# Another model of the two DMA queues in an offline planner that orders the instructions of a transformer trunk

## The chip, the core and the metric

The kernel runs on one core of one Trainium2 chip. The core has TensorE (PE, with its weight loads as PEld), VectorE (DVE), ScalarE (ACT), GpSimd (POOL) and SyncE (SP), each of which works through its own list of instructions in order, and 16 DMA engines that move data. Transfers are issued from two queues here: plain loads by SP, and loads that add to what stands in on-chip memory by POOL. The metric is the device time of one execution in microseconds (us).

## The reference, cut to what matters

```python
D_MODEL, SEQ, DEPTH, D_FF, MEM_TOKENS = 1024, 512, 2, 2816, 256
def swiglu(x, w_gate, w_up, w_down):
    return (jax.nn.silu(x @ w_gate) * (x @ w_up)) @ w_down
for i in range(DEPTH):
    x = layer_norm(ALPHA * x + 0.5 * swiglu(x, ffn_w_gate[i, 0], ffn_w_up[i, 0], ffn_w_down[i, 0]), ...)
    x = layer_norm(ALPHA * x + (mixer_ab if i % 2 == 0 else mixer_c)(x, ...), ...)
    x = layer_norm(ALPHA * x + memory_attn(x, mem, ...), ...)
    x = layer_norm(ALPHA * x + 0.5 * swiglu(x, ffn_w_gate[i, 1], ffn_w_up[i, 1], ffn_w_down[i, 1]), ...)
```

All arrays are float32. Layer 0 mixes tokens by global and windowed attention (`mixer_ab`), layer 1 by neighbourhood attention (`mixer_c`). There are thus eight stages: feed-forward, mixer, memory attention, feed-forward, and the same again.

## The kernel before

Every float32 operand is split into a high part `hi` (a CAST on ACT) and a low part `lo` (a subtraction on DVE), and a product is three matmuls: hi·hi, hi·lo, lo·hi.

A feed-forward stage takes the hidden features in pairs of 256 columns. One pair is called a group. The projections of a group (gate, then up) and the group's share of the down projection are each a 2 by 2 block product done with seven block products, in the order 1, 6, 5, 2, 7, 4, 3 (for down 1, 6, 2, 5, 3, 7, 4). Products of the gate or up half alternate on PE with products of the down share of the group before. Four things recur below, by their names in the instructions (the trace leaves the buffer numbers out):

- `a_…` is the PSUM bank of a gate or up product (three banks in rotation), `d_…` and `t_…` are those of down products, `slab_…` is a tile of 128x1024 in on-chip memory, out of 27 in rotation.
- Product 7 of a half ends in a bank; DVE subtracts it (`t<-a,t`, in `quarters`, `mix(own["c22"], ps, own["c22"], ALU.subtract)`), and product 4 may write that same bank only after this subtraction. This is called the handover here.
- A down share (`down_steps`) loads four quarters of its weights by SP, named 11, 12, 22 and 21. Product 2 uses quarter 21: ACT makes its `hi`, DVE its `lo`.
- Two quarters of the gate weights get their `lo` by a POOL transfer that adds the weights in memory to minus `hi` (`wide_late`, `plus`). They are called adds.

The order is not written by hand. `Graph.record` notes every instruction with its dependencies; `Graph.plan` then plays them through with estimated durations, engine by engine, picks at each step the ready instruction with the smallest key, and hands a tile's buffer on to the next tile in line when its last user has ended. `emit` runs `plan` twice: first with the order of recording as the key, then with the latest start that `deadlines` works out. The instructions are issued in the order that results, and so are the buffers given out. All instructions are issued from one line, so the profile shows L157 for nearly everything.

The part of `plan` that concerns a transfer gives each of the two queues (`kind` is true for SP) a start after its issue, a work time by size, and half of its overlap with the other queue on top; its landing is known as soon as it is issued.

Of the kernel before, what the change touches and what calls it, by code (L numbers as in the profile page):

```python
# [47 lines left out]
class Space:  # L48


    def __init__(self, bufs):
        self.bufs = bufs
        self.queue = []


class Recorder:
# [4 lines left out]

    def __getattr__(self, method):
        return lambda *args, **kw: self.graph.record(self.name, method, args, kw)


class Graph:
# [115 lines left out]
    def plan(self):  # L182

        for info in self.tiles.values():
            info["left"], info["at"], info["behind"] = len(info["users"]), 0.0, None
        now = {e: 0.0 for e in self.ENGINES}
        heaps = {e: [] for e in self.ENGINES}
        ready = {e: [] for e in self.ENGINES}
        free = {s: [(0.0, i, None) for i in range(s.bufs)] for s in self.spaces.values()}
        turn = {s: 0 for s in free}  # L190
        queues = {True: [(0.0, 0.0)], False: [(0.0, 0.0)]}
        held, order, table = [0.0, 0.0], [], None
        for op in self.ops:
            op.wait, op.ready = len(op.deps) + len(op.frees), 0.0

        def release(op, t):
            op.ready = max(op.ready, t)
            op.wait -= 1
            if op.wait == 0:
                heapq.heappush(heaps[op.engine], (op.ready, op.key, op.index, op))  # L200

        def grant(space):

            while turn[space] < len(space.queue) and free[space]:
                info = space.queue[turn[space]]
                turn[space] += 1
                if info["users"]:
                    t, _, info["behind"] = heapq.heappop(free[space])
                    for op in info["users"]:
                        release(op, t)  # L210

        def arrive(e):
            while heaps[e] and heaps[e][0][0] <= now[e]:
                _, key, i, op = heapq.heappop(heaps[e])
                heapq.heappush(ready[e], (key, i, op))

        for op in self.ops:
            if op.wait == 0:
                heapq.heappush(heaps[op.engine], (0.0, op.key, op.index, op))
        for space in free:  # L220
            grant(space)
        while len(order) < len(self.ops):
            best = None
            for e in self.ENGINES:
                arrive(e)
                if ready[e] and e in self.PATIENT:
                    key, _, op = ready[e][0]
                    for at, k, _, _ in heapq.nsmallest(4, heaps[e]):
                        if at < now[e] + op.ns * 0.6 and k < key - self.margin:
                            now[e] = at  # L230
                            arrive(e)
                            break
                if ready[e]:
                    t = now[e]
                elif heaps[e]:
                    t = heaps[e][0][0]
                else:
                    continue
                if best is None or t < best[0]:
                    best = (t, e)  # L240
            assert best, "no instruction can start"
            t, e = best
            if not ready[e]:
                now[e] = t
                continue
            _, _, op = heapq.heappop(ready[e])
            shared = lambda pairs, a, b: sum(max(0.0, min(b, y) - max(a, x)) for x, y in pairs)
            stop = t + op.ns
            if op.port:
                stop += max(0.0, held[e == "vector"] - t)  # L250
                held[e != "vector"] = stop
            if op.table and op.table != table:
                stop += 1290.0
                table = op.table
            lands = stop + self.LATENCY[e]
            if op.dma:
                kind = e == "sync"
                work = 250.0 + op.size / 2**19 * 1700.0 if kind else op.size / 2**19 * (4000.0 if op.adds else 1650.0)
                work *= 1.7 if op.thin else 1.0
                begin = max(t + 1040.0 if kind else stop + 2000.0, queues[kind][-1][1])  # L260
                finish = begin + work + 0.5 * shared(queues[not kind][-6:], begin, begin + work)
                queues[kind].append((begin, finish))
                lands = finish + 790.0
            op.start, op.stop, op.lands, now[e] = t, stop, lands, stop
            order.append(op)
            for u in op.users:
                release(u, stop if e == u.engine == "tensor" else lands)
            for info in op.frees:
                info["left"] -= 1
                info["at"] = max(info["at"], lands)  # L270
                if info["left"] == 0:
                    heapq.heappush(free[info["space"]], (info["at"], len(order), info))
                    grant(info["space"])
        return order

    def deadlines(self, order):
# [1417 lines left out]
```

## Time and profile before

| | |
|---|---|
| time, median of 3 runs (lowest, highest) | 2149.89 us (2148.38, 2151.03) |
| time of the profiled execution | 2146.66 us |
| its span in the profile | 2144.9 us |
| PE busy | 2107.5 us, 98% |
| DVE busy | 1688.0 us, 79% |
| ACT busy | 1268.3 us, 59% |
| POOL busy | 403.6 us, 19% |
| DMA moved | 328.43 MB, mean 153 GB/s |

The profile shows one execution. Spans and waits in it are measured from its first instruction, and the execution's own time is 1.8 us more than its span. A PE that is busy 98% of the time leaves 37.4 us in which it does nothing, the start and the end of the kernel included.

### The profile page before, as it was taken

Reading aid. Unit: us, or ns where it says so; the run is one execution under the profiler, and the core shown is the slowest. Engines: PE = TensorE matmul, PEld = TensorE weight load, DVE = VectorE, ACT = ScalarE, POOL = GpSimd, SP = SyncE. Lnnn points to the kernel's source line nnn. Section 1 sums busy time; section 2 is a strip of 40 time slices with the busy share of each in tenths; the row PEclk is TensorE's granted clock in tenths of the full one; section 3 lists DMA queues with packets and bytes.
Section 4 is the critical chain, followed back from the end, with each engine's and each line's share of the span. In section 5 each row is a group of like instructions: output and inputs, shape, how many; then the busy total and the mean of one; then the engine's idle time right before and its main releaser. Section 6 shows DMA issues by size and latency. Waiting matters only on the chain.

```text
span 2144.9 us, 33922 instructions
## 1 busy us (share of the span) xinstructions
PE 2107.5 (98%) x13056; PEld 1888.2 (88%) x13056; DVE 1688.0 (79%) x2480; ACT 1268.3 (59%) x2019; POOL 403.6 (19%) x473
## 2 busy tenths in 40 slices
PE   9999999999999999999999999999999999999997
PEld 7989988888888999889899989888888888999986
DVE  7778888888747888878889878866568477888787
ACT  5655553699546856455765555447765458655552
POOL 1112105410102211111411111312210013111113
PEclk9999999999999999999999999999999999999999
DMA  7787673003443978785887768346554339678762
GB/s 211 178 200 153 172 189 118 20 11 104 143 138 108 206 156 209 177 197 148 202 166 180 165 158 220 94 128 167 129 162 157 130 107 182 157 183 196 175 167 62
DMA packets 261473, 328.43 MB, mean 153 GB/s; under 512 B 12096, under 2 KB 204224, under 8 KB 261312
## 3 DMA queue, kind: packets, MB, share of 16 engines
q1 hardware_dynamic: 178880, 224.28, 33.0%
q0 software_dynamic: 82144, 101.73, 28.4%
q8 instruction: 103, 1.69, 0.3%
q14 instruction: 58, 0.48, 0.1%
q10 hardware_dynamic: 288, 0.26, 0.0%
HBM read 311.55 MB, written 4.19 MB: 147 GB/s over the span
## 4 chain that ended last, share of the span: by engine, by line
PE 81%; DMA 6%; DVE 5%; ACT 4%; issue 2%; POOL 1%; SPq 0%; DVEq 0%; ACTq 0%; POOLq 0%
PE a L157 49%; PE d L157 19%; PE t L157 13%; DMA slab<-ffn_w_down 5%; DVE slab L157 4%; ACT slab L157 2%; ACT t L157 1%; DVE x L157 1%; DVE t L157 1%; DMA slab<-ffn_w_up 1%; POOL slab L157 1%; ACT raw L157 0%; DMA slab<-t 0%; DMA slab<-ffn_w_gate 0%; ACT xh L157 0%
## 5 line engine op out<-in xcount | busy, mean ns | idle before, releaser
L157 DVE TENSOR_TENSOR slab<-slab,slab 128x1024 fp32r<-128x1024 f32 (+3 forms) x586 | 666.7, 1161 | 125.8 <-ACT slab L157 87.5
L157 ACT CAST slab<-slab 128x1024 fp32r<-128x1024 f32 (+2 forms) x516 | 493.8, 984 | 348.2 <-DVE slab L157 124.8
L157 PE MATMUL a<-slab,slab 128*128 128x256 f32 (+2 forms) x2512 | 624.3, 321 | 0.8 <-DMA slab<-t 0.6
L157 PE MATMUL a<-xh,slab 128*128 128x256 f32 (+2 forms) x2384 | 517.9, 307 | 0.5 <-ACT slab L157 0.5
L157 PE MATMUL a<-raw,slab 128*128 128x256 f32 x2432 | 466.9, 286 | 19.6 <-DVE t L157 18.8
L157 PEld LDWEIGHTS a<-slab,slab 128*128 128x128 f32 x2512 | 449.1, 191 | 38.5 <-ACT t L157 1.3
L157 PE MATMUL d<-slab,slab 128*128 128x512 f32 (+2 forms) x1856 | 450.5, 382 | 0.1
L157 PEld LDWEIGHTS a<-xh,slab 128*128 128x128 f32 x2384 | 395.4, 191 | 26.1 <-ACT slab L157 1.1
L157 PEld LDWEIGHTS a<-raw,slab 128*128 128x128 f32 x2432 | 393.3, 194 | 28.4 <-DVE t L157 22.8
L157 PEld LDWEIGHTS d<-slab,slab 128*128 128x128 f32 x1856 | 329.8, 189 | 57.0 <-DVE slab L157 1.3
L157 PE MATMUL a<-xl,slab 128*128 128x256 f32 (+2 forms) x1192 | 366.6, 308 | 0.0
L157 PEld LDWEIGHTS a<-xl,slab 128*128 128x128 f32 x1192 | 227.4, 191 | 14.3 <-DVE xl L157 0.2
L157 PE MATMUL t<-slab,slab 128*128 128x512 f32 (+1 forms) x840 | 209.1, 389 | 1.0 <-DVE x L157 1.0
L157 DVE TENSOR_TENSOR slab<-raw,slab 128x1024 fp32r<-128x1024 f32 (+2 forms) x148 | 160.7, 1105 | 20.0 <-ACT slab L157 19.9
L157 PEld LDWEIGHTS t<-slab,slab 128*128 128x128 f32 x840 | 150.4, 189 | 27.8 <-issue 1.3
L157 POOL DMA_DIRECT2D slab<-ffn_w_gate x63 | 83.3, 1327 | 411.6 <-DVE slab L157 343.9
L157 DVE TENSOR_TENSOR slab<-t,slab 128x512 fp32r<-128x512 f32 (+2 forms) x223 | 137.6, 638 | 17.1 <-ACT slab L157 16.2
L157 POOL DMA_DIRECT2D slab<-ffn_w_up x63 | 81.2, 1337 | 361.3 <-PE a L157 141.5
L157 ACT CAST slab<-t 128x512 fp32r<-128x512 f32 (+2 forms) x223 | 120.5, 564 | 39.7 <-DVE t L157 14.4
L157 ACT CAST slab<-raw 128x1024 fp32r<-128x1024 f32 (+1 forms) x132 | 124.3, 971 | 30.2 <-PE a L157 8.8
L157 DVE SCALAR_TENSOR_TENSOR x<-d,x 128x512 f32<-128x512 f32 x168 | 114.7, 686 | 20.8 <-PE d L157 20.1
L157 ACT COPY t<-a 128x512 f32<-128x512 f32 (+1 forms) x128 | 69.9, 551 | 75.6 <-PE a L157 46.7
(126 smaller groups left out, 2267.8 us busy)
## 6 DMA issues: line engine op xcount, KB each, us to landing
slab<-ffn_w_gate SPq DMA_DIRECT2D x89, 512.0 KB
slab<-ffn_w_up SPq DMA_DIRECT2D x89, 512.0 KB
slab<-ffn_w_down SPq DMA_DIRECT2D x80, 512.0 KB
slab<-ffn_w_gate POOLq DMA_DIRECT2D x63, 512.0 KB, 8.0
slab<-ffn_w_up POOLq DMA_DIRECT2D x63, 512.0 KB, 7.4
slab<-ffn_w_down POOLq DMA_DIRECT2D x40, 512.0 KB, 8.2
raw<-mem_w_kv SPq DMA_DIRECT2D x16, 1024.0 KB
slab<-t SPq DMA_DIRECT2D x96, 128.0 KB
```

Source lines behind the costliest of these rows:

```text
L157: op.call = lambda: fn(*args, **kw)
```

## The change

The planner's estimate of transfers is replaced; nothing else is edited. A class `Flows` keeps each queue as a line of transfers of which the first is served. Alone, it is served at rate 1; with both queues at work, SP's goes at 0.42 and POOL's at 0.6 of it. A 512 KB load has a work of 1530 (SP), 1515 (POOL) or 2900 (POOL, adding), in the planner's nanoseconds; it can begin 1100 after SP's issue begins or 740 after POOL's ends, costs 710 or 800 more when its queue had stood idle, and lands 700 after its work. A transfer's end is now an event of its own: what waits for it is released when the play reaches that time, and not at its issue.

```diff
+class Flows:
+    READY, WORK, RAMP = (1100.0, 740.0), (1530.0, 1515.0, 2900.0), (710.0, 800.0)
+    SHARE = (0.42, 0.6)
...
+    def begin(self, op, pool):
+        at = op.stop + self.READY[1] if pool else op.start + self.READY[0]
+        work = self.WORK[2 if op.adds else int(pool)] * op.size / 2**19
+        self.queues[pool].append([at, work * (1.7 if op.thin else 1.0), op, False])
...
@@ Graph.plan
-        queues = {True: [(0.0, 0.0)], False: [(0.0, 0.0)]}
+        flows = Flows()
...
+            due = flows.due()
+            if due is not None and (best is None or due <= best[0]):
+                op = flows.finish()
+                op.lands = due + 700.0
+                settle(op)
+                continue
...
-            if op.dma:
-                kind = e == "sync"
-                work = 250.0 + op.size / 2**19 * 1700.0 if kind else op.size / 2**19 * (4000.0 if op.adds else 1650.0)
-                work *= 1.7 if op.thin else 1.0
-                begin = max(t + 1040.0 if kind else stop + 2000.0, queues[kind][-1][1])
-                finish = begin + work + 0.5 * shared(queues[not kind][-6:], begin, begin + work)
-                queues[kind].append((begin, finish))
-                lands = finish + 790.0
             op.start, op.stop, op.lands, now[e] = t, stop, lands, stop
             order.append(op)
...
+            if op.dma:
+                flows.begin(op, e == "gpsimd")
+            else:
+                settle(op)
```

`settle` holds what stood here before: it releases the users of an instruction and hands buffers on.

The set of instructions stays. Their order on DVE and ACT changes at many places, on PE at some forty, on POOL at twelve and on SP at seven. Since buffers are handed on in the order of the play, tiles also get other buffers, so a load can wait for another instruction than before. Three places in the second feed-forward stage, in a gate half whose PE part runs from 878 to 905 us in the trace, show the pattern.

On SP, two quarters of down weights (`slab_1775` is quarter 22, `slab_1792` quarter 21) and the up weights behind them, with the semaphores that each waits for, before:

```order
188 L157 DMA slab_1775<-ffn_w_down 128x2x512 [waits DVE_49]
189 L157 DMA slab_1792<-ffn_w_down 128x2x512 [waits DMAHW7_49,DVE_49]
190 L157 DMA slab_1798<-ffn_w_up 128x4x256 [waits DMAHW0_49,PE_49]
191 L157 DMA slab_1801<-ffn_w_up 128x4x256 [waits DMAHW1_49,DMASW7_49,PE_49]
192 L157 DMA slab_1802<-ffn_w_up 128x4x256 [waits DMAHW2_49,DMASW0_49,DVE_49]
```

and after:

```order
188 L218 DMA slab_1775<-ffn_w_down 128x2x512 [waits DMAHW6_49,DVE_49]
189 L218 DMA slab_1792<-ffn_w_down 128x2x512 [waits DMASW5_49,DMAHW7_49,DMASW2_49,PE_49]
190 L218 DMA slab_1798<-ffn_w_up 128x4x256 [waits DMAHW0_49,PE_49]
191 L218 DMA slab_1801<-ffn_w_up 128x4x256 [waits DMAHW1_49,PE_49]
192 L218 DMA slab_1802<-ffn_w_up 128x4x256 [waits DMASW0_49,DMAHW2_49,PE_49,Activation_49]
```

The order on SP is the same here, but the load of quarter 21 waited for DVE (its count is reached by `slab_1790<-slab_1761,slab_1789`) and now waits for PE (its count is reached by the last matmul of product 1, `a_1764<-xl_84,slab_1758` and its neighbour).

On DVE, around the `lo` of quarter 21 (`slab_1795`) and the handover's subtraction (`t_1696_1777<-a_1769,t_1696_1777`), before:

```order
1040 L157 TENSOR_TENSOR slab_1800<-slab_1750,slab_1799 128x1024
1041 L157 TENSOR_TENSOR slab_1795<-slab_1792,slab_1794 128x1024
1042 L157 SCALAR_TENSOR_TENSOR slab_1586<-t_1791,slab_1586 128x512
1043 L157 TENSOR_TENSOR slab_1804<-slab_1798,slab_1803 128x1024
1044 L157 TENSOR_TENSOR t_1696_1777<-a_1769,t_1696_1777 128x512
1045 L157 TENSOR_TENSOR slab_1811<-slab_1798,slab_1801 128x1024
```

and after:

```order
1038 L218 TENSOR_TENSOR slab_1800<-slab_1750,slab_1799 128x1024
1039 L218 TENSOR_TENSOR t_1740_1821<-t_1703_1784,slab_1745 128x512
1040 L218 TENSOR_TENSOR slab_1795<-slab_1792,slab_1794 128x1024
1041 L218 SCALAR_TENSOR_TENSOR slab_1586<-t_1791,slab_1586 128x512
1042 L218 TENSOR_TENSOR t_1696_1777<-a_1769,t_1696_1777 128x512
1043 L218 TENSOR_TENSOR slab_1804<-slab_1798,slab_1803 128x1024
```

The subtraction moved ahead of the low part of an up quarter (`slab_1804`), and a sum of activations (`t_1740_1821`) moved in ahead of `slab_1795`. Further up, `slab_1790` moved ahead of the sum that needs quarter 22 (`slab_1782<-slab_1781,slab_1775`).

On PE, between product 7 (`a_1769<-raw_1534,slab_1790`) and product 4 (`a_1769<-raw_1534,slab_1778`) of the gate half, before:

```order
4979 L157 MATMUL t_1793<-slab_1786,slab_1787 128x512
4980 L157 MATMUL t_1793<-slab_1785,slab_1787 128x512
4981 L157 MATMUL d_1774<-slab_1794,slab_1796 128x512
4982 L157 MATMUL d_1774<-slab_1795,slab_1796 128x512
4983 L157 MATMUL a_1769<-raw_1534,slab_1778 128x256
```

and after:

```order
4974 L218 MATMUL t_1793<-slab_1786,slab_1787 128x512
4975 L218 MATMUL t_1793<-slab_1785,slab_1787 128x512
4976 L218 MATMUL a_1769<-raw_1534,slab_1778 128x256
4977 L218 MATMUL a_1769<-slab_1536,slab_1778 128x256
4978 L218 MATMUL a_1769<-raw_1534,slab_1779 128x256
```

Two matmuls of down product 2 (`d_1774`) stood between `t_1793` and product 4; they now stand behind product 4 with the other four of that product.

More of the change, by code (lines that the diff above doesn't have):

```diff
@@ L63, in __getattr__, with __init__, advance, due @@
         return lambda *args, **kw: self.graph.record(self.name, method, args, kw)
+class Flows:
+    READY, WORK, RAMP = (1100.0, 740.0), (1530.0, 1515.0, 2900.0), (710.0, 800.0)
+    SHARE = (0.42, 0.6)
+    def __init__(self):
+        self.queues, self.idle, self.clock, self.next = ([], []), [0.0, 0.0], 0.0, None
+    def begin(self, op, pool):
+        at = op.stop + self.READY[1] if pool else op.start + self.READY[0]
+        work = self.WORK[2 if op.adds else int(pool)] * op.size / 2**19
+        self.queues[pool].append([at, work * (1.7 if op.thin else 1.0), op, False])
+        self.next = None
+    def advance(self, until):
+        while True:
+            busy, limit = [], until
+            for k, q in enumerate(self.queues):
+                if q and q[0][0] <= self.clock:
+                    if not q[0][3]:
+                        q[0][3] = True
+                        q[0][1] += self.RAMP[k] if self.idle[k] < q[0][0] else 0.0
+                    busy.append(k)
+                elif q:
+                    limit = min(limit, q[0][0])
+            rate = {k: self.SHARE[k] if len(busy) == 2 else 1.0 for k in busy}
+            ends = [(self.clock + self.queues[k][0][1] / rate[k], k) for k in busy]
+            stop = min([limit] + [z for z, _ in ends])
+            for k in busy:
+                self.queues[k][0][1] -= (stop - self.clock) * rate[k]
+            self.clock = stop
+            for z, k in ends:
+                if z <= stop:
+                    return k
+            if stop >= until:
+                return None
+    def due(self):
+        if not self.queues[0] and not self.queues[1]:
+            return None
+        if self.next is None:
+            kept = self.clock, list(self.idle), [[list(z) for z in q[:1]] for q in self.queues]
+            k = self.advance(1e12)
+            self.next = self.clock, k
+            self.clock, self.idle = kept[0], kept[1]
+            for q, z in zip(self.queues, kept[2]):
+                q[:1] = z
+        return self.next[0]
+    def finish(self):
+        self.due()
+        k = self.next[1]
+        self.advance(self.next[0])
+        self.idle[k], self.next = self.clock, None
+        return self.queues[k].pop(0)[2]
 class Graph:
@@ L221, in plan, with settle @@
             grant(space)
-        while len(order) < len(self.ops):
+        def settle(op):
+            for u in op.users:
+                release(u, op.stop if op.engine == u.engine == "tensor" else op.lands)
+            for info in op.frees:
+                info["left"] -= 1
+                info["at"] = max(info["at"], op.lands)
+                if info["left"] == 0:
+                    heapq.heappush(free[info["space"]], (info["at"], len(order), info))
+                    grant(info["space"])
+        while len(order) < len(self.ops) or flows.due() is not None:
             best = None
@@ L246, in plan @@
             _, _, op = heapq.heappop(ready[e])
-            shared = lambda pairs, a, b: sum(max(0.0, min(b, y) - max(a, x)) for x, y in pairs)
             stop = t + op.ns
@@ L255, in plan @@
             lands = stop + self.LATENCY[e]
-            if op.dma:
-                kind = e == "sync"
-                work = 250.0 + op.size / 2**19 * 1700.0 if kind else op.size / 2**19 * (4000.0 if op.adds else 1650.0)
-                work *= 1.7 if op.thin else 1.0
-                begin = max(t + 1040.0 if kind else stop + 2000.0, queues[kind][-1][1])
-                finish = begin + work + 0.5 * shared(queues[not kind][-6:], begin, begin + work)
-                queues[kind].append((begin, finish))
-                lands = finish + 790.0
             op.start, op.stop, op.lands, now[e] = t, stop, lands, stop
             order.append(op)
[L266 to L273, printed above, removed]
+            if op.dma:
+                flows.begin(op, e == "gpsimd")
+            else:
+                settle(op)
         return order
```

## The prediction

> **What bounds the kernel now.** I read the page first, then who PE waits for, then the chain that ended last, then one wait instruction by instruction.
>
> ```profile
> span 2144.9 us, 33922 instructions
> PE 2107.5 (98%) x13056; PEld 1888.2 (88%) x13056; DVE 1688.0 (79%) x2480; ACT 1268.3 (59%) x2019; POOL 403.6 (19%) x473
> ```
>
> PE is the bound, and a change of order can't shorten its work. It can only take from the 37.4 us in which PE is idle. Who ends that idle time (us in total, times, longest):
>
> ```profile
> PE a L157 <- DVE t L157: 18.8, 11, 3.1
> PE a L157 <- ACT t L157: 0.7, 1, 0.7
> PE a L157 <- DMA slab<-t: 0.6, 2, 0.4
> ```
>
> Half of it is one row: eleven waits of a gate or up product for DVE's `t<-a,t`, the handover. The same question for the stretch 1080 to 1200 us gives the two smallest of them:
>
> ```profile
> PE a L157 <- DVE t L157: 1.7, 2, 0.9
> ```
>
> so nine make 17.1, 1.9 each. The chain says why DVE is late (start, length, what), in the gate half of the second feed-forward stage that the change was shown in:
>
> ```profile
> 876.36 1.23 DVE slab L157
> 877.61 6.31 DMA slab<-ffn_w_down
> ...
> 887.50 1.83 DVE slab L157 x2
> 889.35 6.92 DMA slab<-ffn_w_down
> ...
> 896.34 1.06 ACT slab L157
> ...
> 897.42 1.24 DVE slab L157
> ...
> 900.30 0.70 DVE t L157
> ...
> 901.03 1.01 PE a L157 x6
> ```
>
> A load of quarter 21 starts the moment DVE ends its second instruction (887.50 + 1.83), takes 6.92 us, and ACT, DVE and PE follow it. On ACT and DVE it looks like this (idle time before, and its cause, in brackets):
>
> ```profile
> 889.96 1.05 ACT L157 CAST slab<-slab 128x1024 fp32r<-128x1024 f32 x1 [0.33 <-DVE t L157]
> 896.34 1.05 ACT L157 CAST slab<-slab 128x1024 fp32r<-128x1024 f32 x1 [5.34 <-DMA slab<-ffn_w_down]
> ```
> ```profile
> 892.24 1.22 DVE L157 TENSOR_TENSOR slab<-slab,slab 128x1024 fp32r<-128x1024 f32 x1
> 897.42 1.23 DVE L157 TENSOR_TENSOR slab<-slab,slab 128x1024 fp32r<-128x1024 f32 x1 [3.96 <-ACT slab L157]
> 898.56 0.68 DVE L157 SCALAR_TENSOR_TENSOR slab<-t,slab 128x512 f32<-128x512 f32 x1
> 899.16 1.22 DVE L157 TENSOR_TENSOR slab<-slab,slab 128x1024 fp32r<-128x1024 f32 x1
> 900.30 0.69 DVE L157 TENSOR_TENSOR t<-a,t 128x512 f32<-128x512 f32 x1
> ```
> ```profile
> 896.72 0.28 PE L157 MATMUL a<-raw,slab 128*128 128x256 f32 x1
> 896.84 1.55 PE L157 MATMUL t<-slab,slab 128*128 128x512 f32 x6
> 898.23 0.98 PE L157 MATMUL d<-slab,slab 128*128 128x512 f32 x2
> 901.03 0.39 PE L157 MATMUL a<-raw,slab 128*128 128x256 f32 x1 [1.83 <-DVE t L157]
> ```
>
> Product 7 has ended at 897.0, so the subtraction could run then. It stands in DVE's list behind an instruction that waits for ACT, which waits for the load, and starts at 900.30. Nothing in the subtraction needs the load: a list in order blocks it. The chain has the same load at other places of the kind:
>
> ```profile
> 119.43 7.61 DMA slab<-ffn_w_down
> ...
> 952.51 7.20 DMA slab<-ffn_w_down
> ...
> 1968.09 6.80 DMA slab<-ffn_w_down
> ```
>
> By the old formula a 512 KB load lands 1.04 + 1.95 + 0.79 = 3.8 us after its issue when alone; here it takes 6.7 to 7.6. The old play thus had ACT and DVE go on where they stand still.
>
> **The load of quarter 21.** Its new release is the last matmul of product 1:
>
> ```profile
> 881.06 0.28 PE L157 MATMUL a<-xh,slab 128*128 128x256 f32 x1
> ```
>
> That ends at 881.3; the load before it on SP is out at 877.61, so quarter 21 goes out about 8.0 us before 889.35. At its own 6.92 us it lands at 888.3. Among busier neighbours it may take longer; the longest transfer on the chain is this one:
>
> ```profile
> 1090.28 11.90 DMA slab<-ffn_w_up
> ```
>
> At 11.90 it lands at 893.2, still 3.0 before 896.3. ACT is free at 891.0, so its cast ends by 894.3 at worst. The program has the same exchange, PE for DVE, at each of the nine; at 1182 (one of the small two) the release is 4.5 us earlier.
>
> **The order on DVE.** `slab_1804` (1.14 from start to start) leaves the place before the subtraction, `t_1740_1821` (0.60) comes in. Before that, DVE no longer stands still at quarter 22:
>
> ```profile
> 884.01 1.23 DVE L157 TENSOR_TENSOR slab<-slab,slab 128x1024 f32<-128x1024 f32 x1 [1.57 <-DMA slab<-ffn_w_down]
> ```
>
> Played through with these rows: `t_1703`, `t_1751`, `slab_1787` and `slab_1790` now fill this hole and end near 886.0, the sum with quarter 22 ends at 887.1 (before 885.2), the `lo` of product 6 (`slab_1786`) at 889.5 (before 887.6), `slab_1800` at 891.9, `slab_1795` near 893.7 or, with the slowest load, 895.6, the next accumulation by 896.3. DVE is then idle before 897.0, and the subtraction runs from 897.1 to 897.8.
>
> **The order on PE.** The two `d<-slab,slab` (0.45 from start to start) go behind product 4, so PE is at product 4 at 898.23. The margin is 0.4 us. That such a handover costs nothing is seen in an up half, with six matmuls between and the subtraction on time:
>
> ```profile
> 221.91 1.55 PE L157 MATMUL d<-slab,slab 128*128 128x512 f32 x6
> 223.30 0.28 PE L157 MATMUL a<-raw,slab 128*128 128x256 f32 x1
> ```
> ```profile
> 222.11 0.69 DVE L157 TENSOR_TENSOR t<-a,t 128x512 f32<-128x512 f32 x1 [1.05 <-PE a L157]
> ```
>
> Value of each of the nine: its whole wait. From below it is nothing (the load stays where it was), from above its 1.9; I take the upper end, since even the longest transfer lands in time. The two small ones go for the same reasons (at the one DVE's subtraction moved ahead of two low parts, at the other the load is earlier), and so does the 0.7 behind ACT, at 1103: the copy that PE waits for moved ahead of the cast that waits for the 11.90 us transfer.
>
> **The adds.** They now share their time with one more load. The `lo` of product 2 comes by an add issued here, and by the row of its own stretch lands 8.9 us later, at 887.0:
>
> ```profile
> 878.12 1.28 POOL L157 DMA_DIRECT2D slab<-ffn_w_gate  x1 [1.40 <-ACT slab L157]
> ```
> ```profile
> slab<-ffn_w_gate POOLq DMA_DIRECT2D x1, 512.0 KB, 8.9
> ```
> ```profile
> 889.94 0.40 PE L157 MATMUL a<-xh,slab 128*128 128x256 f32 x2
> ```
>
> PE first reads it at 889.94, so it may be 2.9 us later at no cost. Quarter 22 lands at 883.9 (877.61 + 6.31); until then the add shares as before, and of its last 3.1 us a load beside it can take at most as much again if both get half: 890.1. I take no cost and keep 0.2 for each.
>
> [...] An add alone took 5.9 us (139 us), those in company 8.9, so the trace agrees with the sharing; the planner's own 0.6 and 0.42 are near to half.
>
> **New waits.** PE's order also changes at five places without this pattern: the first gate halves near 765 and 1845, a half near 815, two pairs of heads near 1497 and 1542 whose scores now come earlier among other matmuls. PE does not wait at the first three now, and at the heads the row with 0.6 above is all. Nothing from below; from above, five of the longest of the two waits near 1103 and 1109, 0.9, or 4.5. I take 0.4 each, between nothing and 0.9 and near the two single waits that make the 0.6: 2.0. Start and end keep their instructions, with exchanged neighbours (gate and up banks at the start; `x_4` and `x_5` at the end): nothing. Some loads go out later instead of earlier, most a quarter 12 near 802 (and its like near 1145 and 1882), 5.8 us by the instruction that it now waits for. Here are its issue (the second of two) and the sum that reads it:
>
> ```profile
> 801.89 0.97 SPq L157 DMA_DIRECT2D slab<-ffn_w_down  x2
> ```
> ```profile
> 820.48 1.22 DVE L157 TENSOR_TENSOR slab<-slab,slab 128x1024 f32<-128x1024 f32 x1
> ```
>
> The 18 us between them cover 5.8 and a transfer of 11.90: nothing.
>
> **Sum.** -18.8 - 0.7 + 2.0 = -17.5. Against the profiled execution, 2146.66 - 17.5 = 2129.2. The median of the runs lies 3.23 above the profiled execution, so 2132.4.
>
> **Rivals.**
> 1. The adds are slowed more than by half, and PE waits 1 us at product 2 in ten places: -7.5, so 2142.4. For it: add and loads fill the queues in just these stretches. Against: 2.9 us of room.
> 2. The exchange brings nothing, because the load is served late all the same: DVE's order alone gives 1.14 - 0.60 = 0.54, of which the two matmuls that PE no longer has in front take 0.45. Nine times 0.1: 2149.0, no change. It needs a load of over 15 us (881.3 to 896.3), beyond any row above.
> 3. Slower: `slab_1786` is the place. The down product 6 that needs it starts at 892.58, in a row of its own:
>
> ```profile
> 892.58 0.63 PE L157 MATMUL t<-slab,slab 128*128 128x512 f32 x2
> ```
>
> I have it ready at 889.5. If DVE is held by quarter 22 for 3.1 us more, PE waits; each further us costs ten. The gain is gone at 894.3, and at 895.6 the kernel takes 2146.66 + 3.23 - 17.5 + 30 = 2162. For it: two more instructions stand before it now. Against: quarter 22's release is unchanged.
> 4. The five new places cost 2 us each instead of 0.4: 2140.4.
>
> **How the numbers follow.** My case 0.72 (2127 to 2138: the sum with new waits from nothing to 4.5, the 0.2 of the adds, and some 3 either way for the median's offset); rival 1 0.10; rival 2 0.05; rival 3 0.04; rival 4 0.06; better than 2127, 0.03. A measurement here tells about 0.2%, 4.3 us. The range 2127 to 2143 holds my case, rival 4 and most of rival 1. Faster: 0.72 + 0.10 + 0.06 + 0.03, less 0.01 for the far end of rival 1: 0.90. Same: 0.05 of rival 2 and that 0.01. Slower: rival 3, 0.04.
>
> **What would show it.** Right: PE's wait for `t<-a,t` falls from 18.8 to under 3, ACT's and DVE's brackets of 5.34 and 3.96 are gone or under 1, quarter 21 goes out near 881 within its half, PE's idle time falls to about 20. Wrong: a row of PE waiting for an add or for a DVE `slab` of several us, or the old row still above 9.

## The result, and the profile after

The changed kernel takes 2130.8 us (median of 4 runs, 2130.46 to 2132.42); the kernel before, beside it, 2150.15 (4 runs, 2148.38 to 2151.03). The ratio is 0.9913, its 95% interval 0.9895 to 0.9930. The profiled execution takes 2130.46 us, 16.2 less than that of before.

The head of the page after, and the rows of who PE waits for that answer to those shown (us in total, times, longest):

```profile
span 2128.7 us, 33875 instructions
PE 2101.7 (99%) x13056; PEld 1884.8 (89%) x13056; DVE 1692.7 (80%) x2480; ACT 1270.3 (60%) x2019; POOL 405.7 (19%) x473
```
```profile
PE a L218 <- ACT slab L218: 5.7, 1, 5.7
...
PE d L218 <- DMA slab<-ffn_w_up: 2.5, 2, 1.4
PE a L218 <- DVE t L218: 1.5, 2, 1.0
```

PE's idle time fell from 37.4 to 27.0 us, and its busy time by 5.8: together the 16.2. The row of handovers fell from 18.8 (11 times) to 1.5 (2 times), and neither of these two is one of the old eleven. Two other rows are new: one wait of 5.7 us, and 2.5 us for adds (before, PE waited 0.7 at these two places).

The place that was shown, on SP, ACT, DVE and PE (everything is about 6.2 us earlier by now: product 7's last matmul starts at 890.55, before at 896.72):

```profile
871.44 4.01 SPq L218 DMA_DIRECT2D slab<-ffn_w_down  x2
```
```profile
883.52 2.01 ACT L218 CAST slab<-slab 128x1024 fp32r<-128x1024 f32 x2
```
```profile
886.35 1.22 DVE L218 TENSOR_TENSOR slab<-slab,slab 128x1024 fp32r<-128x1024 f32 x1
888.00 0.69 DVE L218 SCALAR_TENSOR_TENSOR slab<-t,slab 128x512 f32<-128x512 f32 x1 [0.43 <-PE t L218]
890.88 0.69 DVE L218 TENSOR_TENSOR t<-a,t 128x512 f32<-128x512 f32 x1 [2.18 <-PE a L218]
```
```profile
890.55 0.28 PE L218 MATMUL a<-raw,slab 128*128 128x256 f32 x1
890.67 1.55 PE L218 MATMUL t<-slab,slab 128*128 128x512 f32 x6
892.06 0.28 PE L218 MATMUL a<-raw,slab 128*128 128x256 f32 x1
```

The second load of the SP row is quarter 21; its issue ends at 875.45. The second of the two casts on ACT is its own and has no bracket: the load has landed. DVE's first row is its low part, done 3.0 us before product 7's last matmul starts. Now DVE waits for PE (2.18) and not PE for DVE: product 4 follows at 892.06 without a bracket.

The chain of waits shows where the 5.7 us come from, in the third feed-forward stage:

```profile
1067.52 1.29 POOL slab L218
1068.81 0.04 issue
1068.85 0.01 POOLq L218
1068.87 14.16 DMA slab<-ffn_w_gate
1083.03 0.02 issue
1083.05 1.05 ACT slab L218
```

Two adding loads stand behind each other in POOL's queue, and the second one, which PE needs first, takes 14.16 us from issue to landing. The planner's play has it land 8.0 us after its issue: of the 166 adding loads of feed-forward weights, the one that comes latest against the play.

A stretch in which PE is granted half its clock follows that wait. One of the four in the kernel before stands behind the wait at 899 us (columns: stretch, us, PE busy, granted clock, DMA share, GB/s). Before, then after:

```profile
901.84:905.25 3.41, 3.41 (x18) 0.50 0.02 5
```
```profile
1083.71:1090.54 6.83, 6.39 (x29) 0.50 0.30 46
```

In the kernel before, the other three begin at 256.7, 1246.6 and 2041.9, each 2.4 to 3.3 us after the start of a handover wait; the changed kernel has this one only. If half of such a stretch is lost at the granted 0.50, that is 6.8 us before and 3.4 after, an estimate, so 3.4 of the 5.8 us that PE's busy time fell by. The other 2.4 I haven't traced.

### The profile page after: what moved, and what is told of

It is laid out like the page before. It is cut to its first block, busy times and chain, and to the rows that moved or that the text cites. A ratio compares the mean times of both kernels' runs of the same rounds, so it can differ in the third digit from the quotient of the medians.

```text
span 2128.7 us, 33875 instructions
## 1 busy us (share of the span) xinstructions
PE 2101.7 (99%) x13056; PEld 1884.8 (89%) x13056; DVE 1692.7 (80%) x2480; ACT 1270.3 (60%) x2019; POOL 405.7 (19%) x473
## 4 chain that ended last, share of the span: by engine, by line
PE 89%; DMA 4%; DVE 2%; issue 2%; ACT 2%; POOL 1%; SPq 0%; DVEq 0%; POOLq 0%; ACTq 0%
PE a L218 54%; PE d L218 20%; PE t L218 14%; DMA slab<-ffn_w_gate 2%; DVE slab L218 1%; DMA slab<-ffn_w_up 1%; ACT slab L218 1%; DVE x L218 1%; POOL slab L218 1%; DMA slab<-ffn_w_down 0%; SPq L218 0%; ACT t L218 0%; DMA raw<-mem_w_kv 0%; POOL x L218 0%; DMA raw<-x_t 0%
## 5 line engine op out<-in xcount | busy, mean ns | idle before, releaser
L218 PE MATMUL a<-raw,slab 128*128 128x256 f32 x2432 | 462.0, 284 | 1.0 <-DVE t L218 1.0
L218 ACT CAST slab<-t 128x512 fp32r<-128x512 f32 (+2 forms) x223 | 120.5, 565 | 48.6 <-PE t L218 18.8
```

The lines of the kernel that those rows point to most:

```text
L218: op.call = lambda: fn(*args, **kw)
```

## Experiments

The theory on record: the load of quarter 21 left too late, so its release makes the nine waits. The rival: the subtraction stands in the wrong place in DVE's list, and the load's time matters little. Eleven kernels, each timed in turns with the kernel before. `again` in the diffs writes the program out once more, each engine in a given order, buffers handed on as they come free (in late_load as the plan gave them).

| kernel | median us | ratio to before, 95% | PE's wait for DVE `t`: us, times |
|---|---|---|---|
| changed kernel | 2130.8 | 0.9913 (0.9895 to 0.9930) | 1.5, 2 |
| late_load | 2134.65 | 0.9923 (0.9895 to 0.9952) | 1.4, 1 |
| later_load | 2130.16 | 0.9904 (0.9880 to 0.9927) | none |
| latest_load | 2173.53 | 1.0106 (1.0083 to 1.0129) | 26.0, 9 |
| early_load | 2142.85 | 0.9968 (0.9955 to 0.9982) | 16.0, 10 |
| sub_mid | 2136.74 | 0.9939 (0.9922 to 0.9956) | 13.2, 10 |
| both | 2122.03 | 0.9874 (0.9856 to 0.9893) | 0.9, 1 |
| early_sub | 2124.62 | 0.9885 (0.9860 to 0.9911) | 5.1, 4 |
| ahead | 2118.97 | 0.9860 (0.9843 to 0.9877) | none |
| swap_adds | 2127.93 | 0.9892 (0.9872 to 0.9913) | 0.7, 1 |
| land_later | 2132.58 | 0.9923 (0.9906 to 0.9940) | 2.2, 2 |
| no_sharing | 2196.44 | 1.0218 (1.0197 to 1.0239) | 35.8, 15 |

**Is it the time of the load? Three doses on the changed kernel.** The load of quarter 21 waits at nine places for a DVE instruction as well; every engine keeps its order. First the instruction that it waited for in the kernel before (late_load):

```diff
-        for op in order:
-            op.call()
...
+        extra = [(loads[a], lows[b]) for a, b in [(278, 276), (369, 367), (460, 458), (1792, 1790), (1883, 1881), ...]]
+        after = dict(extra)
+        order = self.again(order, extra)
+        made = {}
+        for op in order:
+            made[op] = op.call()
+            if op in after:
+                self.tc.add_manual_dep(made[op].ins, made[after[op]].ins.name, ...)
```

> The changed kernel with every engine's order kept, but at the nine places the load of quarter 21 waits again for the DVE instruction that it waited for before (the low part of product 7's weights), so the buffer exchange alone is undone. By the rows of the changed kernel that instruction ends at 879.9 at the place shown, where the load now goes out near 875: 5 us later. At 6.92 us it lands at 886.8, its cast ends by 887.9, its low part by 889.1, the accumulation by 889.8, and the subtraction can't run before product 7 ends at 890.9. So if the slack is what I think, nothing returns: 2131 us (2129 to 2135), PE's wait for DVE t under 3 us. Rival (the exchanged buffer is the whole of the gain, as the prediction put it): the nine waits return, 17 us, 2148.

Measured 2134.65, at the upper end of the range; by the intervals it isn't told apart from the changed kernel. At eight places nothing returns. At the ninth, at 248 us, the load leaves only 7.5 us before product 7's last matmul, and PE waits 1.4. So the exchanged buffer by itself is not the gain. Next a later instruction, `[(278, 272), (369, 363), ...]`, in later_load:

> The same, but the load of quarter 21 waits for the low part of product 6's weights, which ends at 883.4 at the place shown: 7.5 us before the subtraction can run, as the load before went out 7.65 us before it. If the lateness of the load is the cause: lands 890.3, cast until 891.4, low part until 892.6, accumulation until 893.2, subtraction until 893.9, and PE stands at product 4 from 892.0: about 2 us at nine places, 18 us, 2149 (2144 to 2153), and some stretches at half clock behind the waits come back. Rival (the new order on DVE is the cause, the load's time is not): 2131.

Measured 2130.16: the expectation was wrong, nothing was lost. The place shown, on SP, ACT and DVE:

```profile
885.22 0.37 SPq L218 DMA_DIRECT2D slab<-ffn_w_down  x1
```
```profile
890.12 1.05 ACT L218 CAST slab<-slab 128x1024 fp32r<-128x1024 f32 x1 [3.75 <-DMA slab<-ffn_w_down]
```
```profile
891.20 1.23 DVE L218 TENSOR_TENSOR slab<-slab,slab 128x1024 fp32r<-128x1024 f32 x1 [2.97 <-ACT slab L218]
892.34 0.68 DVE L218 SCALAR_TENSOR_TENSOR slab<-t,slab 128x512 f32<-128x512 f32 x1
892.94 0.68 DVE L218 TENSOR_TENSOR t<-a,t 128x512 f32<-128x512 f32 x1
```

The load went out about as late as in the kernel before (7.1 us before product 7's last matmul, there 7.4), but took 4.8 us instead of 6.9, and the subtraction has no bracket: in time by a hair. The add beside the load tells why, before and here (KB, us from issue to landing):

```profile
slab<-ffn_w_down POOLq DMA_DIRECT2D x1, 512.0 KB, 7.7
```
```profile
slab<-ffn_w_down POOLq DMA_DIRECT2D x1, 512.0 KB, 9.4
```

Before, this add was issued 1.5 us ahead of the load, here 0.3 behind it. The pair takes 14.6 us there and 14.2 here: whoever is second seems to pay. (That is read from one place, not tried.) So the load had to be held back further, behind an instruction that ends 4.7 us before product 7's last matmul: `[(278, 286), (369, 377), ...]` in latest_load.

> The changed kernel's order on every engine, with the load of quarter 21 held back at the nine places until the DVE instruction that ends 4.7 us before product 7's last matmul starts. Held back to 7.1 us before it (later_load) the load took 3.6 to 5.2 us, its cast began 2.2 to 3.6 us before product 7's end, and nothing was lost. At 4.5 us the cast now begins at about -0.2 us, where it began in the kernel before (-1.05 to 0.12); the subtraction starts 2.8 us after it, ends at 3.3, and PE stands at product 4 at 1.5. If the time at which the load lands is the cause: 1.8 us at nine places, 16 us, 2146 (2142 to 2156, the upper end if the loads take 6.9 us or half-clock stretches come back with the waits). Rival (the new order on DVE made the gain, and the load's time doesn't count): 2131.

Measured 2173.53, above the range that I gave. On DVE and PE at the place shown:

```profile
908.35 1.23 DVE L218 TENSOR_TENSOR slab<-slab,slab 128x1024 fp32r<-128x1024 f32 x1 [6.23 <-ACT slab L218]
909.50 0.68 DVE L218 SCALAR_TENSOR_TENSOR slab<-t,slab 128x512 f32<-128x512 f32 x1
910.10 0.68 DVE L218 TENSOR_TENSOR t<-a,t 128x512 f32<-128x512 f32 x1
```
```profile
910.83 0.39 PE L218 MATMUL a<-raw,slab 128*128 128x256 f32 x1 [2.92 <-DVE t L218]
```

The nine waits are back, 2.2 to 3.5 us each: the loads took up to 6.0 us, and the casts began 0.7 to 1.4 us after product 7's last matmul started at eight places. In the new order, too, the subtraction is late when the load lands late. The clock comes on top: the mean granted clock of the profiled execution is 0.990, that of the changed kernel 0.997, by an estimate from these means and the spans (2171.7 and 2128.7 us) some 15 us more lost. With 26.0 us of waits where 16 were expected, that puts it above the range.

**One half alone, the other half alone, both.** On the kernel before. early_load keeps every order and only lets the nine loads take the first buffer that comes free:

```diff
...
+        first = [op for op in order if op.engine == "sync" and op.srcs[0] == "ffn_w_down" and number(op.outs[0]) in [278, 369, ...]]
+        order = self.again(order, first)
```

> The kernel before with every engine's order kept; only the nine loads of quarter 21 get a buffer that comes free earlier (last read by a PE matmul ahead of product 1), so they go out right behind quarter 22, near 878 at the place shown: 18 us before product 7's end instead of 7.4. The order on DVE and PE is the old one, in which the subtraction starts 4.0 us after the cast of quarter 21 and PE stands at product 4 at 2.0 us, so a cast that starts by -2.7 us costs nothing. If the load's time is what the change gained by: with 6.9 to 9.4 us the load has landed when ACT is free (-5.7), the nine waits go, and 2150 - 17 - up to 6 of half-clock stretches = 2127 to 2133. Rival (the change's new order on DVE and PE was needed too): waits of 1 us or more stay at the nine places, 2138 to 2150. Second rival (the loads now take from the adds beside them, and PE waits for these): a new row of PE waits for adds, 2135 to 2145.

Measured 2142.85: a third of a per cent, and 16.0 of the 18.8 us stay. PE's idle time as a whole did not fall at all in the profiled execution (37.8 us), since a wait of 3.0 for ACT's `t` came at 1809, far from the nine places. The rival was right. ACT and DVE at the place shown:

```profile
886.67 2.00 ACT L157 CAST slab<-slab 128x1024 fp32r<-128x1024 f32 x2
889.77 0.60 ACT L157 ACTIVATE t<-a 128x512 f32<-128x512 f32 x1 [1.10 <-PE a L157]
895.17 1.05 ACT L157 CAST slab<-slab 128x1024 fp32r<-128x1024 f32 x1 [4.80 <-DMA slab<-ffn_w_up]
```
```profile
891.88 0.68 DVE L157 SCALAR_TENSOR_TENSOR slab<-t,slab 128x512 f32<-128x512 f32 x1
896.25 1.22 DVE L157 TENSOR_TENSOR slab<-slab,slab 128x1024 fp32r<-128x1024 f32 x1 [3.70 <-ACT slab L157]
897.40 0.68 DVE L157 TENSOR_TENSOR t<-a,t 128x512 f32<-128x512 f32 x1
```

Product 7's last matmul starts at 893.71 here. Quarter 21 is cast at 887.63 without a wait, and DVE is through with its low part and the accumulation at 892.56. Then comes `slab_1804`, the low part of the next load in line, the up quarter. Its cast has to wait for that load until 895.17, and the subtraction stands behind it as it stood behind quarter 21. There are two blocked instructions in front of it, not one.

sub_mid moves the subtraction ahead of that second one only, and the two matmuls on PE as the change does:

```diff
+        for n in [278, 369, ...]:
...
+            dve.remove(sub)
+            dve.insert(front, sub)
...
+            pe[at:at] = early
+        order = self.again(order, {"vector": dve, "tensor": pe})
```

> The kernel before with the other half of the change's pattern alone: at the nine places the subtraction stands ahead of the low part of the up quarter, but still behind the low part of quarter 21 and the accumulation, and the two matmuls of down product 2 stand behind product 4. The load of quarter 21 stays as late as it was: its cast begins 1.05 us before to 0.1 us after product 7's last matmul, the subtraction 2.8 us after that and 0.7 long, and PE stands at product 4 at 1.5. So each wait keeps about 1.3 us (12 in all, of 18), and PE gains some 0.9 at each place: 2142 (2136 to 2146; no wait is long enough for a half-clock stretch any more, so up to 6 of the gain can be the clock). Rival (the low part of the up quarter, blocked by its own load, was the only thing in the way): the waits go, 2125.

Measured 2136.74: 13.2 us of waits stay, about what I expected. More of its gain is PE's busy time (2101.8, before 2107.5), at a mean granted clock of 0.998 where before has 0.995. Then both edits:

> The kernel before with both halves of the pattern, early_load and sub_mid together, and nothing else of the change. If the two halves are needed together: no wait at the nine places, as in early_sub, 2125 (2121 to 2130), which is 15 us or more below either half alone. Rival (something else in the change's order is needed too): waits of 1 us or more stay, 2135 or more.

Measured 2122.03, and the row of handovers is down to

```profile
PE a L157 <- DVE t L157: 0.9, 1, 0.9
```

The halves take 2.8 and 5.6 us out of that row, together they take 17.9. Neither half clears the row; both are needed, since there are two blocks in a row. In time the halves bring 5.3 and 13.3 us, both 28.0; a part of that is the clock, with means of 0.996, 0.998 and 0.998 granted in the profiled executions, and 0.995 in that of before.

**The block itself.** early_sub leaves the load as late as it was and moves the subtraction ahead of both: `dve.insert(k, sub)`, where `k` is the place of quarter 21's low part. The two matmuls of down product 2, which read that low part, go behind product 4 here too.

> The kernel before, its load of quarter 21 as late as it was, but at the nine places the subtraction stands in DVE's list ahead of the low part that waits for the load, and the two matmuls of down product 2 on PE behind product 4. If a blocked list is the whole mechanism: the subtraction runs when product 7 ends (897.0 at the place shown) and ends at 897.7, PE reaches product 4 at 897.8: the nine waits go without any earlier load, 2150 - 17 = 2133 (2128 to 2137, the lower end if half-clock stretches behind the waits go too). Rival (the load itself is what PE needs soon after): PE then waits for the low part or for a later one behind it, 1 to 2 us at each place, 2142 to 2150.

Measured 2124.62, below the range. At the place shown, on DVE:

```profile
893.36 0.69 DVE L157 TENSOR_TENSOR t<-a,t 128x512 f32<-128x512 f32 x1 [3.83 <-PE a L157]
893.97 1.22 DVE L157 TENSOR_TENSOR slab<-slab,slab 128x1024 fp32r<-128x1024 f32 x1
```

The nine waits are gone with loads that take 6.8 to 7.9 us. At product 4 PE didn't need what the loads carry; it needed the subtraction. Four handovers of other halves are left (5.1 us). ahead treats these and a copy on ACT alike:

```diff
...
+        for line, out, src, front in [(dve, 312, 301, 336), (dve, 494, 483, 519), (dve, 2113, 2109, 2127), (dve, 3553, 3545, 3571), (act, 2054, 2109, 2120)]:
+            take = first(line, out, src)
+            line.remove(take)
+            line.insert(line.index(first(line, front)), take)
```

> early_sub, and the same move at five more places: four subtractions on DVE and one copy on ACT that PE waits for go ahead of an instruction that waits for a load (waits of 1.57, 1.87, 0.89, 0.80 and 0.48 us in the trace of early_sub). If a blocked list is the mechanism there too: 5.6 us less than early_sub, and its one half-clock stretch, which follows the 1.87, goes as well: 2124.6 - 5.6 - 1.7 = 2117 (2114 to 2121). Rival (PE is short of what the blocked load carries a moment later): 2122 to 2126.

Measured 2118.97, as expected: the fastest kernel here, with the old planner and the loads where they were. Its interval (0.9843 to 0.9877) lies below that of the changed kernel, each taken against the kernel before.

**The new wait.** swap_adds exchanges the two adds at 1067 us on POOL in the changed kernel:

```diff
...
+        first, second = [next(op for op in pool if op.dma and number(op.outs[0]) == n) for n in (2091, 2037)]
+        k = pool.index(first)
+        pool.remove(second)
+        pool.insert(k, second)
...
```

> The changed kernel with two adding loads exchanged on POOL at one place (1067 us, third feed-forward stage): the one that ACT and PE wait for at 1078 first. If its place behind the other is what made the new wait of 5.9 us: it lands at about 1078.6 instead of 1083.0 and PE waits about 1.5 us, and the stretch at half clock behind the wait (3.4 us lost) may go with it: 2131 - 4.4 = 2126.5, or 2123 with the clock. Rival (the two share one queue and the transfers around them are slow whoever is first): the other add is then late for PE, which needs it 2.9 us after the first: no more than 1 us gained, 2130.

Measured 2127.93. The 5.7 is gone, and the other add is waited for instead:

```profile
PE a L218 <- DMA slab<-ffn_w_gate: 1.8, 1, 1.8
```

The profiled execution is 4.0 us shorter; the intervals of the two kernels overlap, so the size is known only roughly. The place in the queue was most of that wait.

land_later lets the planner see all landings 0.5 us later:

```diff
-                op.lands = due + 700.0
+                op.lands = due + 1200.0
```

> The changed kernel's planner with every landing 0.5 us later (1200 for 700). In the changed kernel the new wait of 5.9 us hangs on an add that the play lands 8.0 us after its issue and the chip 14.2 us, and the two waits of 1.1 and 1.4 on adds that it lands 8.8 and the chip 9.3 to 11.6. With later landings the play puts the add of 1078 us first in its queue. If the play's adds are too fast: the 5.9 falls to at most 1.8, as in swap_adds, and the rest stays: 2127 (2122 to 2130). Rival (any other play of this size loses as much elsewhere): 2131 to 2140.

Measured 2132.58: the rival was right. The wait for ACT's cast is gone, but the adds for the up weights now cost more, other waits come, and the mean granted clock of the profiled execution is 0.995 where the changed kernel's is 0.997:

```profile
PE d L218 <- DMA slab<-ffn_w_up: 6.3, 3, 3.3
```

**Which part of the planner.** no_sharing keeps `Flows`, events and lengths, with `SHARE = (1.0, 1.0)`:

> The changed kernel's planner with SHARE at 1 and 1: the same two servers and landings as events, but a transfer isn't slowed by one on the other queue. If the knowledge that transfers beside each other land late is the part of the change that matters, the play falls back to the old pattern (the load behind product 7's weights on DVE, the subtraction behind the low part of an up quarter) and the nine waits return: 2148 (2143 to 2155). Rival (events, or the lengths and latencies, are what matters): 2131.

Measured 2196.44. The old pattern is back, as the first theory has it, but with 15 handovers waited for instead of 11, and two waits for adds, the longer of 3.9 us: far above my range, and above the kernel before, whose planner counted half of the time that transfers spend side by side. More than a third of what it lost on the kernel before is the clock, by an estimate from the mean granted clocks of the profiled executions and their spans: 0.987 over 2189.8 us there, 0.995 over 2144.9 before, some 18 us.

```profile
PE a L218 <- DVE t L218: 35.8, 15, 3.7
PE d L218 <- DMA slab<-ffn_w_up: 6.5, 2, 3.9
```

So the gain hangs on sharing being counted; events and lengths without it are worse than what they replaced. Other rates than 0.42 and 0.6 weren't tried.

## Why the prediction was right or wrong

The time, 2130.8 for 2132.4, came out within 2 us because three misses cancel. New waits are 9.1 us (27.0 of idle time, less the 17.9 that 37.4 - 18.8 - 0.7 leaves), not 2.0: +7.1. PE's busy time fell by 5.8; the prediction had said that a change of order can't shorten PE's work, and no step had this. And the median lies 0.3 above the profiled execution, not 3.23: -2.9. 2132.4 + 7.1 - 5.8 - 2.9 = 2130.8. That they cancel is luck.

- **The handovers: right in size.** All eleven waits are gone, 18.8 us, and the 0.7 behind ACT at 1103 too. (The 1.9 of each of the nine is a mean: one is 3.1, eight are 1.5 to 1.8.) ACT's and DVE's brackets of 5.34 and 3.96 are gone. The issue of quarter 21 ends 15.1 us before product 7's last matmul starts (875.45 to 890.55); predicted were 15.4 (8.0 before 889.35, so 881.3, to 896.72).
- **The order on DVE: right.** Played through by hand, `slab_1795` was to end 3.0 us before product 7's last matmul starts (893.7), the subtraction to run 0.4 after it: measured 2.98 before (886.35 + 1.22) and 0.33 after.
- **The cause: right in kind, wrong in its parts, and this is the step that failed.** That a blocked list holds up the subtraction is confirmed by early_sub. But I gave the load of quarter 21 the whole 1.9 at each place, and `slab_1804` its own 1.14 us. early_load shows what the load is worth alone: 2.8 of the 18.8. `slab_1804` isn't 1.14 us of work in front of the subtraction; it waits for a load of its own, and takes the first one's place as the block. The rows that could have told it were in the trace of before, on SP and ACT:

```profile
889.35 0.37 SPq L157 DMA_DIRECT2D slab<-ffn_w_down  x1
890.18 1.09 SPq L157 DMA_DIRECT2D slab<-ffn_w_up  x2
```
```profile
897.85 1.99 ACT L157 CAST slab<-slab 128x1024 fp32r<-128x1024 f32 x2
```

The up load goes out 0.8 us behind quarter 21, and `slab_1803`, its cast, is the next cast on ACT. At the 6.92 us of quarter 21 it lands at 897.1, an estimate: no sooner than product 7 ends. I moved one instruction out of the line without asking what the next would itself wait for.

- **The rivals.** Rival 2 didn't come: none of the nine loads took 15 us, each was being cast within 9.5 us of its issue. But no rival had a second block in the list, by which in early_load the waits stayed with all nine loads in time. Rivals 1 and 3 didn't come either: at the nine places PE waits for no add and for no DVE `slab`.
- **The adds: right at the places of the pattern, wrong elsewhere.** PE waits for no add at product 2 of the nine halves, so the 0.2 each didn't appear. But I looked for slow adds only beside the moved loads. They cost 5.7 us at 1078 and 1.9 more at 726 and 1800, where PE's order or POOL's had changed: the "row of PE waiting for an add" that I had named as a sign of failure, at a place that I hadn't listed.
- **The new waits: mis-sized and mostly misplaced.** This is the term of the sum that was furthest off: 2.0 for 9.1, with 0.4 at each of five places. Of the 9.1, 5.7 came at 1078, 1.9 at the adds and 1.5 at two new handovers. The 5.7 came at none of the five places, and swap_adds shows that one exchange on POOL made most of it.
- **The clock: left out.** Four half-clock stretches of 3.41 us before, one of 6.83 after: 3.4 us of gain, by the estimate above. The other 2.4 of PE's busy time stay open.
- **The median's offset.** The prediction took the 3.23 of the kernel before for the changed one, where it is 0.3. The kernel before varies from 2143.7 to 2158.7 us over its runs here, with a mean granted clock from 0.996 down to 0.993. Its profiled execution, with four stretches, was one of the faster ones; the changed kernel's runs lie within 2 us.

## What to carry to other kernels

An instruction that the bound engine waits for is late by everything ahead of it in its own list, so ask of each one in front which load it waits for, down to the second and third: taking away the first block shows only the next (in early_load 16.0 of the 18.8 us stayed). The cheapest cure is to move the wanted instruction ahead of all that waits for transfers (what PE reads of the instructions passed over then has to stand later on PE too, as the two matmuls did); that beat both planners here (ahead, 2118.97 us), without any better knowledge of the transfers. And when a planner's model gets better on the average, look where it is still most wrong: here that one place made PE wait 5.7 us, beside a gain of 19.4.

## What the runs showed of the hardware

In the traces of before and after, the granted clock is 1.00 or 0.50, and the stretches at 0.50 come behind waits or the end of PE's work. Before has it at 0.50 for 3.41 us each at 256.72, 901.84, 1246.58 and 2041.89, and from 2137.46 on, when PE is done; after for 6.83 us at 1083.71, and from 2121.36 on, when PE is done. The starts lie 645.12, 344.74, 795.31 and 95.57 us apart in the one, 1037.65 in the other: 189, 101, 233, 28 and 304 times 3.413. Ahead of the stretch at 256.72, matmuls of 128x256 start 0.12 us apart (255.77 and 255.89), in it 0.21 (256.92 and 257.13).

In the 3.41 us before the four stretches of before, PE is idle for 1.83, 1.92, 1.83 and 1.76 us, and for all 3.41 before that of after. The other seven handover waits of before are followed by none: 1.70 (at 192), 1.68 (1306), 1.52 (1978), 0.90 and 0.81, but also 1.83 (963) and 3.14 (129). In spans of 3.41 us laid end to end from the starts above, these two are divided, the 1.83 as 0.63 and 1.20 and the 3.14 as 1.74 and 1.39; but so is the 5.71 of after, and of its spans the one with 1.86 us idle (from 1076.88) is followed by full clock, the next by half. In the stretch of 6.83, PE is idle for 0.44 us in the first half and the clock stays at 0.50 in the second. What decides it, no run shows. The profiled executions of both and ahead, whose longest waits are 1.6 and 1.4 us, have a mean granted clock of 0.998 and 0.999.

The clock is a part of why taking away nine waits brought more than their sum. The profiled execution of early_sub is 21.0 us shorter than that of before: 14.2 of idle time (13.7 in the row of handovers) and 6.8 of PE's busy time. By the mean granted clocks and the spans, 0.998 over 2123.9 us and 0.995 over 2144.9, some 6 of these are the clock, an estimate that the rounding of the means leaves open by 1 or 2. The kernel before varies from run to run, too: its mean granted clock, 0.996 to 0.993, is lowest in its slowest runs. By an estimate from these two means that is some 6 us of the 15 between them, and only one of these runs was traced.
